# Lower parts of the weights and S5's two products move from GpSimd to VectorE in a one-core mixer kernel

## The chip, the core and the metric

The kernel runs on one core of a Trainium2 chip. The core has several engines, each with a queue of its own that it works off in order: TensorE multiplies matrices (PE in the profile's rows, PEld for its weight loads), VectorE (DVE) and ScalarE (ACT) do elementwise work, GpSimd (POOL) does elementwise work as well, and SyncE (SP) issues transfers. The metric is the device time of one execution in microseconds (us); lower is better. Times of one kernel are compared by the median of several runs.

## The reference

Two layers run one after the other on 512 tokens of width 1024. The first is a mixer of an S5 state-space branch and a gated convolution, followed by a squared-ReLU MLP. The second is a gated delta rule (forward and backward, with a context of 256 tokens) beside a Fourier mixer, followed by a mixture of 32 experts. What matters here is the first mixer and the dense products with its weights:

```python
proj = jnp.einsum('bsd,de->bse', xn, w_in) + b_in
u_ssm, c_bgate, c_cgate, c_val, g_ssm, g_conv = jnp.split(proj, SPLIT_POINTS, axis=-1)
y_ssm = s5_branch(u_ssm, ...)            # complex diagonal recurrence along the tokens
z = jax.nn.gelu(y_ssm)
y_a = (z @ w_glu_a) * jax.nn.sigmoid(z @ w_glu_b)
y_b = (c_bgate * causal_short_conv(c_cgate * c_val, conv_w, conv_b)) @ w_conv_out
merged = jax.nn.sigmoid(g_ssm) * y_a + jax.nn.sigmoid(g_conv) * y_b
return merged @ w_out
```

S5 has 32 groups of 64 complex states, 2048 states in all. The kernel does the complex recurrence as a rotation and two real scans: inputs are turned by cos and sin of the state's phase, scanned with a real decay, and turned back. The turning back takes four products per tile: sr = cos·zr − sin·zi and si = cos·zi + sin·zr.

## The kernel before, in words

Activations lie with features on the 128 partitions and the 512 tokens along the row. A dense product goes through its weights in blocks of 128 output columns (`dense`, with the weights from `weights`). Each fp32 weight block of 128x1024 is split in two: ScalarE casts it to a high part `wh` (L125), and `lsub` subtracts that from the block and so makes the low part `wl` (L126). TensorE then runs 24 matmuls per block: activations' high and low parts against `wh` (L130, L131) and the high part against `wl` (L138). `wh` and `wl` have two buffers each, and the loaded block `w`, which holds two blocks of 128 columns, has two as well. `lsub` is VectorE in most of the kernel. It is GpSimd in two stages: from the start of S5 until S5 is drained and its pools are closed, and from the start of `x_path` (the second layer's projections, its delta rule and its output projection) to the end.

S5 (`s5`) is a generator of 16 steps j, each for a tile of 128 states, with three pieces per step. `dense` calls for the next piece after its blocks (`fill`): two pieces after each block of the gate and value projections, one after a block of the bg projection and of the convolution's output projection, none in the gc blocks that come last. A piece's work goes to these lines: phase `fr` on VectorE (L442, L445, L446), its sin and cos on ScalarE (L448 to L450), two matmuls `bu` (L455), then VectorE's turning (L460 to L465) and scans (L468, L469), and the turning back (L473 to L478), of which L474 and L477 are on GpSimd. After each fourth step, 16 matmuls `y` (L486) read the four steps' sr and si. Beside it VectorE does the convolution of the gated branch (L547 to L557) and the low parts of its activations (L153).

In the second layer the lower parts are made beside the convolution taps of the projections (L1248) and a matrix inverse (L887 to L930), both on VectorE.

The order of the instructions on each engine is not written out by hand: a scheduler sets it when the program is built, and it moves instructions of independent pieces past one another.

Of the kernel before, what the change touches and what calls it, by code (L numbers as in the profile page):

```python
# [15 lines left out]
P = 128  # L16
# [13 lines left out]
def f(t):  # L30
    return t.bitcast(F32)
# [53 lines left out]
class Kern:  # L85
# [31 lines left out]
    def weights(self, w, r0, kt, c0, cols):  # L117
        nc = self.nc
        W = self.wp.tile([P, 8, 256], F32, tag="w", bufs=2, name=self.nm("w"))
        nc.sync.dma_start(  # L120
            W[:, :kt, :cols], w[r0:r0 + kt * P, c0:c0 + cols].rearrange("(k p) c -> p k c", p=P))
        for c in range(0, cols, P):
            H = self.wp.tile([P, 8, P], F32R, tag="wh", bufs=2, name=self.nm("wh"))
            L = self.wp.tile([P, 8, P], F32R, tag="wl", bufs=2, name=self.nm("wl"))
            nc.scalar.copy(H[:, :kt], W[:, :kt, c:c + P])  # L125
            self.lsub.tensor_sub(L[:, :kt], W[:, :kt, c:c + P], f(H[:, :kt]))  # L126
            yield H, L

    def accH(self, ps, H, aH, aL, k, sl=slice(None)):
# [85 lines left out]
    def setup(self):  # L215
        nc = self.nc
        ins = self.ins
        self.cp = self.pool("const")
        self.wes = ExitStack()
        self.es.enter_context(self.wes)  # L220
        self.wp = self.pool("wts", es=self.wes, side="right")
        self.pp = self.pool("ps", space=PSUM, es=self.ppes)
        self.lsub = nc.vector
        pk = self.cp.tile([P, ins["c_pack"].shape[1]], F32, name="pk")
        ni = COFF["ident"][1]
        assert COFF["ident"][0] == 0
        nc.gpsimd.dma_start(pk[:, :ni], ins["c_pack"][:, :ni])
        self.c = {k: pk[:, o:o + n] for k, (o, n) in COFF.items()}
        self.ident = self.c["ident"]
        self.ones = self.cp.tile([P, P], F32, name="ones")  # L230
        nc.vector.memset(self.ones, 1.0)
        self.pk = pk
# [195 lines left out]

    def s5(self, sp, u, zH, zL):
        nc = self.nc  # L430
        V, G = nc.vector, nc.gpsimd
        S = [P, T]

        def t(tag, bufs=1):
            return sp.tile(S, F32, tag=tag, bufs=bufs, name=self.nm(tag))

        st = {}
        for j in range(16):

            fr = t("fr")  # L440
            n = t("m1")
            V.tensor_tensor(fr.rearrange("p (a b) -> p a b", b=16),  # L442
                            self.fa[:, j, :32].unsqueeze(2).broadcast_to([P, 32, 16]),
                            self.fa[:, j, 32:].unsqueeze(1).broadcast_to([P, 32, 16]), op=ALU.add)
            V.tensor_scalar(n, fr, MAGIC, MAGIC, op0=ALU.add, op1=ALU.subtract)  # L445
            V.tensor_sub(fr, fr, n)  # L446
            sn, cs = t("sn", 2), t("cs", 2)
            nc.scalar.activation(sn, fr, AF.Sin, scale=2 * math.pi * (1 - 2e-7))  # L448
            nc.scalar.activation(fr, fr, AF.Abs)
            nc.scalar.activation(cs, fr, AF.Sin, scale=-2 * math.pi, bias=self.halfpi)  # L450
            jr = slice(32 * (j % 4), 32 * (j % 4) + 32)
            bu = []
            for i in range(2):
                b = self.pp.tile(S, F32, tag="q", bufs=4, name=self.nm("bu"))
                nc.tensor.matmul(b, self.bbT[jr, i, j // 4], u[jr, j // 4], start=True, stop=True,  # L455
                                 tile_position=(32 * (j % 4), 0))
                bu.append(b)
            yield
            m1, m2, m3, m4 = t("m1"), t("m2"), t("m3"), t("m4")
            V.tensor_mul(m1, cs, bu[0])  # L460
            V.tensor_mul(m4, sn, bu[0])
            V.tensor_mul(m2, sn, bu[1])
            V.tensor_mul(m3, cs, bu[1])
            V.tensor_add(m1, m1, m2)
            V.tensor_sub(m3, m3, m4)  # L465
            zr, zi = m2, m4
            mg = self.mag[:, j:j + 1].broadcast_to(S)
            V.tensor_tensor_scan(zr, mg, m1, 0.0, op0=ALU.mult, op1=ALU.add)  # L468
            V.tensor_tensor_scan(zi, mg, m3, 0.0, op0=ALU.mult, op1=ALU.add)  # L469
            yield  # L470
            sr, si = t("sr", 4), t("si", 4)
            n1, n2 = m1, m3
            V.tensor_mul(sr, cs, zr)  # L473
            G.tensor_mul(n1, sn, zi)  # L474
            V.tensor_sub(sr, sr, n1)
            V.tensor_mul(si, cs, zi)
            G.tensor_mul(n2, sn, zr)  # L477
            V.tensor_add(si, si, n2)  # L478
            st[j % 4] = (sr, si)
            if j % 4 == 3:  # L480
                i4 = j // 4
                y = self.pp.tile(S, F32, tag="q", bufs=4, name=self.nm("y"))
                for i in range(2):
                    for a in range(4):
                        ja = slice(32 * a, 32 * a + 32)
                        nc.tensor.matmul(y[ja, :], self.ccT[:, i, i4, ja], st[a][i], start=(i == 0), stop=(i == 1),  # L486
                                         tile_position=(0, 32 * a), skip_group_check=True)
                ys = t("m1")
                z = t("m2")
                V.scalar_tensor_tensor(ys, u[:, i4], self.v["ssm_d"][:, i4:i4 + 1], y, op0=ALU.mult, op1=ALU.add)  # L490
                nc.scalar.activation(z, ys, AF.Gelu_apprx_tanh)
                self.split(z, zH[:, i4], zL[:, i4])
            yield

    def block1(self):
        nc, ins = self.nc, self.ins
        V, A = nc.vector, nc.scalar
# [24 lines left out]
        sp = self.pool("s5", es=es)  # L522
        zz = a2.tile([P, 2, 4, T], F32R, tag="Z", name="zz")
        zH, zL = zz[:, 0], zz[:, 1]
        self.lsub = nc.gpsimd
        self.fillers.append(self.s5(sp, u, zH, zL))

        cH = ap_.tile(B, F32R, tag="D", name="cH")
# [45 lines left out]
        self.dense(w_in, xH, xL, take_gc, 4608, D)  # L574
        self.drain_fillers()
        es.close()
        self.lsub = nc.vector
        lp = tp = self.pool("late", es=aes)
        ya = lp.tile(B, F32, tag="G", name="ya")
        st = {}  # L580
# [53 lines left out]
        zr = tp.tile([P, D], F32, name="zr")  # L634
# [536 lines left out]
    def x_path(self):  # L1171

        nc, ins = self.nc, self.ins
        V, A, M, Q = nc.vector, nc.scalar, nc.tensor, nc.gpsimd
# [6 lines left out]
        w = ins["w_in_2"][0]  # L1181
        cw = self.v["conv_w_2"]
        x2d = self.dr.tile([P, KD, T], F32, name="x2d")
        self.lsub = Q

        def y_():
            return hp.tile([P, T], F32, tag="sq", bufs=3, name=self.nm("y"))
# [5 lines left out]
        G = self.cp.tile([P, 8], F32, name="gx")  # L1193
# [949 lines left out]
```

## Time and profile before

| what | value |
|---|---|
| median of 3 runs | 1989.0 us (1984.17 to 1991.39) |
| profiled execution, its own time | 1987.15 us |
| its span on the core | 1985.4 us |
| mean granted TensorE clock | 0.932 |
| TensorE busy | 1765.2 us, 89% of the span |
| VectorE busy | 1114.9 us, 56% |
| ScalarE busy | 585.3 us, 29% |
| GpSimd busy | 321.8 us, 16% |

All busy times are of the one profiled execution. They are means over stages that have different limits: the S5 stage lies at about 85 to 392 us of the span, the gc blocks after it end at about 430 us, the second layer's projections and delta rule lie at about 1030 to 1242 us, its output projection at about 1342 to 1400 us, and the experts after that.

### The profile page before, as it was taken

Reading aid. Unit: us, or ns where it says so; the run is one execution under the profiler, and the core shown is the slowest. Engines: PE = TensorE matmul, PEld = TensorE weight load, DVE = VectorE, ACT = ScalarE, POOL = GpSimd, SP = SyncE. Lnnn points to the kernel's source line nnn. Section 1 sums busy time; section 2 is a strip of 40 time slices with the busy share of each in tenths; the row PEclk is TensorE's granted clock in tenths of the full one; section 3 lists DMA queues with packets and bytes.
Section 4 is the critical chain, followed back from the end, with each engine's and each line's share of the span. In section 5 each row is a group of like instructions: output and inputs, shape, how many; then the busy total and the mean of one; then the engine's idle time right before and its main releaser. Section 6 shows DMA issues by size and latency. Waiting matters only on the chain. (4 is left out here: it accounts for less than half of the span.)

```text
span 1985.4 us, 24482 instructions
## 1 busy us (share of the span) xinstructions
PE 1765.2 (89%) x9169; PEld 1143.1 (58%) x9169; DVE 1114.9 (56%) x2231; ACT 585.3 (29%) x989; POOL 321.8 (16%) x210
## 2 busy tenths in 40 slices
PE   6778889699999999999998988999698898899985
PEld 4545556376676788777775665887333333333332
DVE  4889898833454665594466689573532323233225
ACT  3222324242343244332344633233411111111112
POOL 0434344420000000000012222003110111111000
PEclk9888889799999999999998889899799999999997
DMA  4111111138556333222231211006599999989993
GB/s 137 63 64 43 43 64 64 42 126 280 210 170 242 120 95 115 67 86 85 64 105 65 64 43 56 13 12 245 206 382 413 413 402 413 389 309 413 412 406 136
DMA packets 150266, 351.15 MB, mean 177 GB/s; under 512 B 20435, under 2 KB 107036, under 8 KB 130235
## 3 DMA queue, kind: packets, MB, share of 16 engines
q1 hardware_dynamic: 135533, 302.52, 41.2%
q0 software_dynamic: 9008, 33.58, 4.6%
q10 hardware_dynamic: 5534, 12.54, 1.7%
q8 instruction: 115, 1.88, 0.4%
q14 instruction: 76, 0.62, 0.1%
HBM read 339.63 MB, written 19.15 MB: 181 GB/s over the span
## 5 line engine op out<-in xcount | busy, mean ns | idle before, releaser
L125 ACT CAST wh<-w 128x1024 fp32r<-128x1024 f32 (+1 forms) x184 | 179.3, 975 | 407.7 <-PE acc L131 340.2
L126 POOL TENSOR_TENSOR wl<-w,wh 128x1024 fp32r<-128x1024 f32 (+1 forms) x76 | 184.7, 2434 | 621.0 <-PE acc L138 375.7
L1733 PE MATMUL gu<-ew,moe 128*64 128x512 f32 x1024 | 262.5, 639 | 14.2 <-DMA ew<-in_w_gate_dram 8.7
L126 DVE TENSOR_TENSOR wl<-w,wh 128x1024 fp32r<-128x1024 f32 (+1 forms) x108 | 123.2, 1141 | 118.7 <-PE acc L138 89.2
L1733 PEld LDWEIGHTS gu<-ew,moe 128*64 128x64 f32 x1024 | 73.9, 145 | 147.8 <-issue 120.4
L130 PE MATMUL acc<-xH,wh 128*128 128x512 f32 x352 | 151.3, 430 | 0.3 <-ACT wh L125 0.3
L131 PE MATMUL acc<-xL,wh 128*128 128x512 f32 x352 | 148.0, 420 | 0.0
L1742 DVE TENSOR_TENSOR moe<-gu,moe 64x512 f32<-64x512 f32 x32 | 21.8, 683 | 201.7 <-ACT moe L1741 136.2
L1758 PE MATMUL dn<-ew,hT 128*64 128x512 f32 x512 | 119.0, 608 | 0.5 <-ACT hT L1751 0.5
L130 PE MATMUL acc<-fH,wh 128*128 128x512 f32 x256 | 103.5, 405 | 0.4 <-ACT fH L152 0.4
L130 PE MATMUL acc<-gH,wh 128*128 128x512 f32 x256 | 103.2, 403 | 0.0
L1751 ACT COPY hT<-tr 128x128 f32<-128x128 f32 x64 | 13.9, 269 | 299.1 <-PE tr L1748 283.3
L131 PE MATMUL acc<-fL,wh 128*128 128x512 f32 x256 | 102.0, 398 | 0.0
L131 PE MATMUL acc<-gL,wh 128*128 128x512 f32 x256 | 102.0, 398 | 0.0
L138 PE MATMUL acc<-xH,wl 128*128 128x512 f32 x352 | 94.4, 412 | 6.5 <-DVE wl L126 3.7
L130 PEld LDWEIGHTS acc<-xH,wh 128*128 128x128 f32 x352 | 71.7, 204 | 42.3 <-issue 19.4
L1703 POOL DMA_INDIRECT yd<-moe,sx x31 | 32.0, 1033 | 339.2 <-DVE moe L1766 168.9
L131 PEld LDWEIGHTS acc<-xL,wh 128*128 128x128 f32 x352 | 71.5, 203 | 21.1 <-issue 5.5
L138 PEld LDWEIGHTS acc<-xH,wl 128*128 128x128 f32 x352 | 69.0, 197 | 24.0 <-DVE wl L126 4.2
L1758 PEld LDWEIGHTS dn<-ew,hT 128*64 128x64 f32 x512 | 36.4, 139 | 68.7 <-issue 63.8
L1766 DVE SCALAR_TENSOR_TENSOR moe<-dn,wv,moe 128x512 f32<-128x512 f32 x32 | 24.0, 751 | 89.5 <-PE dn L1758 64.6
L130 PE MATMUL acc<-hxH,wh 128*128 128x512 f32 x160 | 70.9, 447 | 2.1 <-DVE y L1248 2.1
(706 smaller groups left out, 3458.7 us busy)
## 6 DMA issues: line engine op xcount, KB each, us to landing
ew<-in_w_up_dram SPq DMA_DIRECT2D x64, 1024.0 KB
ew<-in_w_gate_dram SPq DMA_DIRECT2D x64, 1024.0 KB
ew<-in_w_down_dram SPq DMA_DIRECT2D x64, 1024.0 KB
w<-in_w_in_dram SPq DMA_DIRECT2D x36, 1024.0 KB
w<-in_w_ff_dram SPq DMA_DIRECT2D x32, 1024.0 KB
wm<-in_w_mod_dram POOLq DMA_DIRECT2D x24, 1024.0 KB, 6.5
xt<-in_x_dram SPq DMA_DIRECT2D x8, 512.0 KB
w<-in_w_conv_out_dram SPq DMA_DIRECT2D x4, 1024.0 KB
```

Of the source, the lines that this page charges most:

```text
L125: nc.scalar.copy(H[:, :kt], W[:, :kt, c:c + P])
L126: self.lsub.tensor_sub(L[:, :kt], W[:, :kt, c:c + P], f(H[:, :kt]))
L130: self.nc.tensor.matmul(ps, H[:, k], aH[:, k, sl], start=(k == 0), stop=False)
L131: self.nc.tensor.matmul(ps, H[:, k], aL[:, k, sl], start=False, stop=False)
L138: nc.tensor.matmul(ps, L[:, k], aH[:, k, sl], start=False, stop=(k == kt - 1))
L1703: nc.gpsimd.indirect_dma_start(out=self.yd.rearrange("r (m c) -> (r m) c", m=m), out_offset=bass.IndirectOffsetOnAxis(ap=sx, axis=0), in_= ...
L1733: mm = M.matmul(gu[64 * j:64 * j + 64], xs[:, k, s0:s0 + 64], ws[2 * (k // 4) + j][:, k % 4], start=(n == 0), stop=(n == 7), tile_position ...
L1742: V.tensor_mul(gh[:64], gu[:64], gh[64:])
L1751: put(hT[:, q:q + 2], pt[:, 64 * q:64 * q + 128].rearrange("p (k s) -> p k s", k=2))
L1758: M.matmul(dn[64 * j:64 * j + 64], hT[:, q], ws[4 + q // 2][:, q % 2, 512 * j:512 * j + 512], start=(q == 0), stop=(q == 3), tile_position ...
L1766: V.scalar_tensor_tensor(y, dn, wsl, m5, op0=ALU.mult, op1=ALU.mult)
```

## The change

All lower parts are made by VectorE: `lsub` is gone. In S5 the products L474 and L477 go to VectorE too. That moves 76 lower parts (60 of 128x1024 elements, 16 of 128x512) and 32 products of 128x512 from GpSimd to VectorE. Nothing is removed or added, and no buffer changes its size. In the changed kernel the line numbers are one lower in `s5`, two lower in the first layer after it, and three or four lower in the second.

```diff
             nc.scalar.copy(H[:, :kt], W[:, :kt, c:c + P])
-            self.lsub.tensor_sub(L[:, :kt], W[:, :kt, c:c + P], f(H[:, :kt]))
+            nc.vector.tensor_sub(L[:, :kt], W[:, :kt, c:c + P], f(H[:, :kt]))
             yield H, L
...
-        self.lsub = nc.vector
         pk = self.cp.tile([P, ins["c_pack"].shape[1]], F32, name="pk")
...
-        V, G = nc.vector, nc.gpsimd
+        V = nc.vector
...
             V.tensor_mul(sr, cs, zr)
-            G.tensor_mul(n1, sn, zi)
+            V.tensor_mul(n1, sn, zi)
             V.tensor_sub(sr, sr, n1)
             V.tensor_mul(si, cs, zi)
-            G.tensor_mul(n2, sn, zr)
+            V.tensor_mul(n2, sn, zr)
             V.tensor_add(si, si, n2)
...
-        self.lsub = nc.gpsimd
         self.fillers.append(self.s5(sp, u, zH, zL))
...
         es.close()
-        self.lsub = nc.vector
         lp = tp = self.pool("late", es=aes)
...
         x2d = self.dr.tile([P, KD, T], F32, name="x2d")
-        self.lsub = Q
```

The first place is VectorE's queue in the S5 stage, from a step's second scan to the next steps' first products. Names are tiles with the number of their use: `sr`, `si` are the step's results, `sn`, `cs` its sin and cos, `m_...` its scratch, `fr` the next step's phase, `magk` the decay, `wl`, `w` and `wh` low part, block and high part. A row ends with the engines that the instruction waits for. Before:

```order
L469 SCALAR_TENSOR_TENSOR m_214_1236<-magk,m_213_1235 128x512 [waits DVE_49]
L473 TENSOR_TENSOR sr_1278<-cs_1193,m_212_1234 128x512 [waits DVE_49]
L476 TENSOR_TENSOR si_1279<-cs_1193,m_214_1236 128x512 [waits DVE_49]
L475 TENSOR_TENSOR sr_1278<-sr_1278,m_211_1233 128x512 [waits DVE_49,Pool_49]
L478 TENSOR_TENSOR si_1279<-si_1279,m_213_1235 128x512 [waits DVE_49,Pool_49]
L442 TENSOR_TENSOR fr_1286<-fa 128x512
```

GpSimd's queue before, around the same step:

```order
L126 TENSOR_TENSOR wl_1429<-w_1366,wh_1428 128x1024 [waits PE_49,Activation_49]
L474 TENSOR_TENSOR m_211_1233<-sn_1192,m_214_1236 128x512 [waits DVE_49,Activation_49,Pool_49]
L477 TENSOR_TENSOR m_213_1235<-sn_1192,m_212_1234 128x512 [waits Pool_49]
L126 TENSOR_TENSOR wl_1487<-w_1484,wh_1486 128x1024 [waits DMAHW5_49,PE_49,Activation_49]
L126 TENSOR_TENSOR wl_1531<-w_1484,wh_1530 128x1024 [waits PE_49,Activation_49]
```

VectorE's queue in the changed kernel, at the same step:

```order
L468 SCALAR_TENSOR_TENSOR m_214_1236<-magk,m_213_1235 128x512 [waits DVE_49]
L472 TENSOR_TENSOR sr_1278<-cs_1193,m_212_1234 128x512 [waits DVE_49]
L473 TENSOR_TENSOR m_211_1233<-sn_1192,m_214_1236 128x512 [waits DVE_49]
L475 TENSOR_TENSOR si_1279<-cs_1193,m_214_1236 128x512
L474 TENSOR_TENSOR sr_1278<-sr_1278,m_211_1233 128x512 [waits DVE_49]
L476 TENSOR_TENSOR m_213_1235<-sn_1192,m_212_1234 128x512
L441 TENSOR_TENSOR fr_1286<-fa 128x512
L477 TENSOR_TENSOR si_1279<-si_1279,m_213_1235 128x512 [waits DVE_49]
L444 TENSOR_SCALAR m_223_1287<-fr_1286 128x512 [waits DVE_49]
L126 TENSOR_TENSOR wl_1369<-w_1366,wh_1368 128x1024 [waits DMAHW4_49,PE_49]
L445 TENSOR_TENSOR fr_1286<-fr_1286,m_223_1287 128x512 [waits DVE_49]
L126 TENSOR_TENSOR wl_1429<-w_1366,wh_1428 128x1024 [waits PE_49,Activation_49]
```

The two products now stand between the step's other products, the waits for GpSimd are gone, and two lower parts stand behind the step, ahead of the next step's turning. They wait for TensorE (the buffer of the low part) and for ScalarE (the high part).

The second place is VectorE's queue in the delta rule, where steps of the inverse (`inv`) alternate with convolution taps (`y`, from `pad` and the tap's weight in `vt`). Before:

```order
L916 TENSOR_TENSOR inv_7657<-inv_7657 128x252 [waits DVE_49]
L1248 SCALAR_TENSOR_TENSOR y_8280<-pad_7117,vt_538,y_8280 128x512 [waits DVE_49]
L918 TENSOR_TENSOR inv_7657<-inv_7657 128x18x14 [waits DVE_49]
L1248 SCALAR_TENSOR_TENSOR y_8280<-pad_7117,vt_538,y_8280 128x512 [waits DVE_49]
L916 TENSOR_TENSOR inv_7657<-inv_7657 128x255 [waits DVE_49]
```

In the changed kernel:

```order
L913 TENSOR_TENSOR inv_7657<-inv_7657 128x252 [waits DVE_49]
L1244 SCALAR_TENSOR_TENSOR y_8280<-pad_7117,vt_538,y_8280 128x512 [waits DVE_49]
L915 TENSOR_TENSOR inv_7657<-inv_7657 128x18x14 [waits DVE_49]
L1244 SCALAR_TENSOR_TENSOR y_8280<-pad_7117,vt_538,y_8280 128x512 [waits DVE_49]
L913 TENSOR_TENSOR inv_7657<-inv_7657 128x255 [waits DVE_49]
L126 TENSOR_TENSOR wl_8400<-w_8346,wh_8399 128x1024 [waits PE_49,Activation_49]
```

A lower part now stands in the inverse's chain and waits there for TensorE and ScalarE.

## Rows read from the trace of the kernel before

**Rows 1.** The page's 40 slices of the span, busy tenths of two engines.

```profile
DVE  4889898833454665594466689573532323233225
POOL 0434344420000000000012222003110111111000
```

**Rows 2.** Windows: stretch, its length, each engine's busy time with instructions, and more.

```profile
core 0: us, PE busy (x) PEld busy (x) DVE busy (x) ACT busy (x) POOL busy (x), PEclk, DMA share, GB/s
45.00:85.00 40.00, 29.28 (x112) 19.96 (x111) 30.16 (x113) 10.02 (x12) 11.36 (x4) 0.86 0.22 74
85.00:316.00 231.00, 187.34 (x639) 119.50 (x638) 212.43 (x230) 58.98 (x77) 97.66 (x46) 0.86 0.17 54
316.00:362.00 46.00, 44.22 (x175) 32.15 (x174) 39.31 (x35) 17.89 (x25) 22.35 (x10) 1.00 0.20 68
362.00:392.00 30.00, 14.47 (x45) 7.46 (x45) 27.59 (x26) 8.17 (x11) 14.22 (x7) 0.69 0.11 36
392.00:430.00 38.00, 37.18 (x151) 28.43 (x148) 15.14 (x12) 16.60 (x19) 14.55 (x9) 0.93 0.31 112
1030.00:1150.00 120.00, 104.29 (x436) 73.38 (x435) 80.50 (x184) 59.57 (x100) 30.67 (x12) 0.84 0.19 64
1150.00:1242.00 92.00, 76.82 (x420) 56.69 (x422) 87.02 (x142) 30.66 (x46) 26.33 (x11) 0.94 0.17 53
1342.00:1400.00 58.00, 55.90 (x260) 42.53 (x259) 21.23 (x32) 17.55 (x29) 21.64 (x18) 0.94 0.60 212
```

**Rows 3.** What TensorE waits for at 85 to 392: total us, times, longest.

```profile
PE y L486 <- DVE sr L475: 27.2, 7, 7.6
PE bu L455 <- DVE m L461: 13.3, 4, 6.4
```

**Rows 4.** Timeline of VectorE and GpSimd at 213 to 218: start, duration, instruction.

```profile
213.83 1.75 DVE L475 TENSOR_TENSOR sr<-sr,m 128x512 f32<-128x512 f32 x1
215.50 2.86 DVE L478 TENSOR_TENSOR si<-si,m 128x512 f32<-128x512 f32 x1
...
213.32 1.71 POOL L477 TENSOR_TENSOR m<-sn,m 128x512 f32<-128x512 f32 x1
214.99 2.82 POOL L126 TENSOR_TENSOR wl<-w,wh 128x1024 fp32r<-128x1024 f32 x1
```

**Rows 5.** VectorE's groups at 85 to 392: busy us, mean ns | idle before.

```profile
L478 DVE TENSOR_TENSOR si<-si,m 128x512 f32<-128x512 f32 x16 | 39.1, 2442 | 0.0
L475 DVE TENSOR_TENSOR sr<-sr,m 128x512 f32<-128x512 f32 x16 | 28.2, 1760 | 1.2 <-POOL m L474 1.2
L476 DVE TENSOR_TENSOR si<-cs,m 128x512 f32<-128x512 f32 x16 | 27.2, 1701 | 0.0
...
L469 DVE TENSOR_TENSOR_SCAN m<-magk,m 128x512 f32<-128x512 f32 x16 | 19.1, 1195 | 0.0
...
L461 DVE TENSOR_TENSOR m<-sn,bu 128x512 f32<-128x512 f32 x16 | 10.9, 679 | 0.0
```

**Rows 6.** GpSimd's groups at 85 to 392.

```profile
L126 POOL TENSOR_TENSOR wl<-w,wh 128x1024 fp32r<-128x1024 f32 x31 | 82.8, 2676 | 72.1 <-PE acc L138 42.7 <-ACT wh L125 21.5 <-ACT m L491 6.9
L477 POOL TENSOR_TENSOR m<-sn,m 128x512 f32<-128x512 f32 x16 | 27.1, 1695 | 0.0
```

**Rows 7.** VectorE's lower parts at 430 to 1000, where `lsub` is VectorE.

```profile
L126 DVE TENSOR_TENSOR wl<-w,wh 128x1024 fp32r<-128x1024 f32 x83 | 101.3, 1220 | 92.2 <-PE acc L138 68.8 <-ACT wh L125 21.3 <-PE acc L287 2.1
```

**Rows 8.** VectorE's groups in the delta rule at 1150 to 1242.

```profile
L1248 DVE SCALAR_TENSOR_TENSOR y<-pad,vt,y 128x512 f32<-128x512 f32 x39 | 35.2, 902 | 0.0
...
L887 DVE TENSOR_TENSOR m<-m,beta 128x1024 f32<-128x1024 f32 x2 | 4.5, 2309 | 0.0
L1248 DVE SCALAR_TENSOR_TENSOR y<-pad,vt,acc 128x512 f32<-128x512 f32 x6 | 4.4, 738 | 2.2 <-PE acc L1246 2.2
L904 DVE SCALAR_TENSOR_TENSOR inv<-m,pk,inv 128x512 f32<-128x512 f32 x2 | 3.5, 1786 | 0.0
...
L888 DVE TENSOR_TENSOR m<-m,pk 128x1024 f32<-128x1024 f32 x2 | 2.3, 1212 | 0.0
```

## The prediction

> **What bounds the kernel now.** I read the 40 slices first, to see where the two engines of the change are busy together. GpSimd works in slices 2 to 9, where VectorE stands at 8 or 9 tenths, in slices 21 to 25, and lightly after that [rows 1]. So the change touches three stretches, and the mean VectorE share of the table (56%) says nothing about them. The windows give each stretch its limit [rows 2]. At 85 to 316 us, the S5 loop, VectorE is busy 212.4 of 231 us and TensorE 187.3. At 316 to 362 TensorE has 44.2 of 46: it sets the pace there. At 362 to 392, when the projections have run ahead and only S5 is left, VectorE has 27.6 of 30 and TensorE 14.5. At 392 to 430 TensorE has 37.2 of 38. In the delta rule, at 1150 to 1242, VectorE has 87.0 of 92 and TensorE 76.8; at 1030 to 1150 neither is full (80.5 and 104.3 of 120); at 1342 to 1400 TensorE has 55.9 of 58. TensorE's waits in the S5 stage say the same: 27.2 us of them end with VectorE's `sr` and 13.3 us with VectorE's turning, which frees the buffer that the next `bu` is written to [rows 3].
>
> So VectorE binds in two of the S5 stretches and in the delta rule, and the change gives it more to do there. What decides is how much of its busy time is work. The groups answer that [rows 5]. L461, a product of 128x512 with one input in PSUM, takes 679 ns. L476, L475 and L478 are also one product, one difference and one sum of 128x512, and take 1701, 1760 and 2442 ns, without idle time ahead of them. In the timeline L475 ends at 215.58 and GpSimd's L477 at 215.03; L478 ends at 218.36 and GpSimd's lower part at 217.81 [rows 4]. Both times VectorE's instruction ends 0.55 us after GpSimd's, as if it could begin only when GpSimd had finished. I read this as VectorE being held while GpSimd reads the memory that both use, if VectorE's own instruction takes two operands from there; L461, with an operand in PSUM, is not held.
>
> [...]
>
> **The change part by part.** Prices first. A lower part on VectorE takes 1.220 us [rows 7], against 2.676 on GpSimd [rows 6]. A product takes 0.68 us (L461), against 1.695. An instruction starts about 0.08 us before the one ahead ends (L475 starts at 213.83, lasts 1.75, and L478 starts at 215.50), so what one adds to VectorE's queue is 1.14 and 0.60 us.
>
> Added in the S5 stage: 31 lower parts and 32 products (two in each of 16 steps; 63 GpSimd instructions in the three windows together). That is 31 x 1.14 + 32 x 0.60 = 35.3 + 19.2 = 54.5 us.
>
> Removed there: the held time. The three slow groups alone have 39.1 + 28.2 + 27.2 - 3 x 10.9 = 61.8 us of it. For all groups I take VectorE's busy time less what its instructions would take unheld: 0.60 us each, and 0.52 more for each of the 32 scans (1.195 against 0.68). This is an estimate, since a few instructions are shorter or longer. At 85 to 316: 212.4 - 230 x 0.60 - 24 x 0.52 = 62. At 316 to 362: 39.3 - 35 x 0.60 - 4 x 0.52 = 16. At 362 to 392: 27.6 - 26 x 0.60 - 4 x 0.52 = 10. Together 88 us.
>
> The net by stretch, GpSimd's instructions being 22 lower parts and 24 products in the first, 6 and 4 in the second, 3 and 4 in the third:
> At 85 to 316: 25.1 + 14.4 = 39.5 added, 62 removed, net -22.5. TensorE has 43.7 idle us there to let the loop shorten.
> At 316 to 362: 9.2 added, 16 removed; net -7 for VectorE, but TensorE is the limit. I take 0.
> At 362 to 392: 5.8 added, 10 removed, net -4. TensorE only waits there.
> At 392 to 430: five lower parts, 5.7 us, into 22.9 us that VectorE is idle. 0; with no cover +6.
> At 45 to 85, the preparation of S5: four lower parts, 4.6 us, into 9.8 idle us of VectorE. 0, bounds -4 (some instructions held there too) and +5.
>
> The delta rule. At 1150 to 1242 there are nine lower parts, 10.3 us. Held: taps L1248 take 902 ns against 738 for those with an operand in PSUM, 39 x 0.164 = 6.4; L887 2 x (2.309 - 1.212, by L888 of the same size) = 2.2; L904 2 x (1.786 - 0.738) = 2.1; 10.7 in all [rows 8]. The inverse has other instructions that look drawn out, which I don't count. I take -2, with bounds of -8 and +10 (all nine on the path, nothing given back). At 1030 to 1150 there are eight, 9.1 us, beside 39.5 idle us of VectorE: 0, and +9 without that cover. The output projection at 1342 to 1400 has the 16 half-sized ones and one whole, below 17 x 1.14 = 19.4 us, beside 36.8 idle us: 0.
>
> What else moves. No transfer is added and no queue of transfers is passed. But a lower part now stands in VectorE's queue with S5's instructions behind it, and waits there for ScalarE's cast and for TensorE to free the buffer; before, GpSimd waited alone. In the new order they stand mostly between a step's phase and its turning, where VectorE waited for sin and cos anyway. How long they will wait the trace of before cannot show. It is bounded by 0 and by 1.11 us each, the idle time ahead of a lower part where VectorE makes them now (92.2 / 83) [rows 7]. I take a value near 0, because in that stretch VectorE has nothing else to do and so idles without cost, while in S5 it is the late one and finds its buffers free.
>
> The sum: -22.5 - 4 - 2 = -28.5 us on the profiled execution's 1987.15, which makes 1958.7. That execution lies 1.85 us under the median of 1989.0, so the same against the median is 1960.5; I say 1959. The experts behind it are limited by transfers that start with the output projection (transfers' share 0.60 there), and I take it that they move ahead as a whole.
>
> **The rivals.**
> (1) The loop gains, but half of it is lost again. TensorE's matmuls against the low part now depend on the engine that is late, where GpSimd made them early; a wait of TensorE for `wl` takes the place of that for `sr`. GpSimd's only 2.676 us speak for it, since `wl` was rarely late before. 0.5 us for each of 22 lower parts is 11 us: -28.5 + 11 = -17.5, and with the delta rule at +5 instead of -2, -10: about 1978.
> (2) Slower: VectorE blocks. If each lower part of S5 and the projections (31 + 17) waits 1.11 us at the head of the queue with the recurrence behind it, that is 53 us, and the result +25: about 2013. The point from which it decides is 28.5 / 48 = 0.6 us each. For it: 42.7 us of GpSimd's idle time ahead of its lower parts end with TensorE's matmuls and 21.5 with ScalarE's cast [rows 6], so they do arrive just behind these. Against it: GpSimd took each as soon as it could, VectorE comes to them later.
> (3) GpSimd takes real load off a full engine, and the slow VectorE instructions are slow for another reason. Then 31 x 1.22 + 32 x 0.68 = 59.6 us come on top in S5: about 2045. Against it are the two ends 0.55 us apart and L461. [...]
> (4) More gain. The lower parts fill the gaps in which VectorE waits for sin and cos, so that its 18.6 idle us at 85 to 316 shrink too, say by 13, and the second stretch and the delta rule give their full -7 and -8: -22.5 - 13 - 7 - 4 - 8 = -54.5, about 1934.
>
> **How the numbers follow.** My forecast (a gain of 18 to 45 us): 0.57. Rival 1: 0.19, half of it faster by over 0.5% (10 us, about what a measurement of this kernel can tell from no change) and half within. Rival 2: 0.14, of which 0.11 by more than 10 us. Rival 3: 0.03. Rival 4: 0.07. Faster: 0.57 + 0.09 + 0.07 = 0.73; within: 0.10 + 0.03 = 0.13; slower: 0.14. The range leaves out most of rivals 3 and 4 and the upper end of rival 2: 1937 to 1990. My forecast's own is 1944 to 1971.
>
> **What would show it right or wrong.** Right: L475, L476 and L478 (one line lower then) at about 680 ns each; lower parts in S5 at about 1.2 us on VectorE; its busy time in the loop some 20 us less; TensorE's waits for `sr` and for the turning smaller by as much; the gc blocks reached some 26 us earlier. Rival 1 would show as TensorE waiting for `wl` from VectorE, rival 2 as VectorE idle ahead of L126 inside the loop, by TensorE or ScalarE. The forecast fails if the three groups stay at 1.7 us or more, if the loop stays as long with a shorter busy VectorE, or if the delta rule grows by as much as S5 gives.

## The result and the profile after

The changed kernel took 1919.8 us (median of 4 runs, 1917.9 to 1925.5) against 1990.2 for the kernel before on the same occasions. The ratio is 0.9651, with a 95% interval of 0.9616 to 0.9687: 70 us faster. The forecast was 1959 with a range of 1937 to 1990, so the time lies 17 us below the range. The direction was right, the size less than half of what came.

The changed kernel's slices, the same rows as [rows 1]:

```profile
DVE  4899999334545654864558797565432232232315
POOL 0000000000000000000000000000001011011100
```

The slices show GpSimd out of the S5 loop and of the delta rule, and the stretch in which VectorE is full has become shorter (six slices at 8 or 9 tenths, where there were seven).

To compare stage by stage I cut both traces at the same work: S5 from its first phase to its last `si`, and from there to the first product that reads S5's result. First the kernel before, then the changed one, in the windows view (columns as in [rows 2]):

```profile
79.10:393.00 313.90, 252.17 (x878) 162.73 (x877) 283.45 (x296) 89.33 (x118) 137.49 (x64) 0.87 0.17 54
393.00:433.90 40.90, 40.84 (x164) 31.54 (x165) 14.14 (x12) 17.22 (x20) 14.10 (x8) 0.95 0.29 104
```

```profile
74.60:332.40 257.80, 230.48 (x860) 152.89 (x858) 245.31 (x357) 87.29 (x114) 0.00 (x0) 0.94 0.19 62
332.40:374.10 41.70, 41.70 (x177) 32.65 (x176) 14.06 (x18) 18.45 (x22) 2.00 (x3) 1.00 0.37 128
```

VectorE runs 61 instructions more in the S5 loop and is busy 38 us less. It is idle 12.5 us there, where it was idle 30.4. The loop is 56 us shorter. Where the profiled executions' 61.7 us of difference in span come from, by the same cuts: 4.5 us ahead of S5's first phase, 56.1 in the loop, -0.8 in the gc blocks behind it, 0.5 up to the second layer's first product, 10.3 from there to the output projection, and -8.9 (given back) in the output projection and the experts. That last stretch lasts 644 to 654 us from one profile to another in the runs below, with the changed kernel and with kernels that change nothing in it, so I don't count its difference as an effect; the medians, 70 us apart, are nearer to the 70.6 gained up to there.

The groups that answer to [rows 5], one line lower now, and the lower parts beside them:

```profile
L126 DVE TENSOR_TENSOR wl<-w,wh 128x1024 fp32r<-128x1024 f32 x30 | 36.4, 1216 | 1.3 <-PE acc L138 1.3
...
L468 DVE TENSOR_TENSOR_SCAN m<-magk,m 128x512 f32<-128x512 f32 x16 | 19.1, 1196 | 0.0
...
L475 DVE TENSOR_TENSOR si<-cs,m 128x512 f32<-128x512 f32 x16 | 10.9, 681 | 0.0
L474 DVE TENSOR_TENSOR sr<-sr,m 128x512 f32<-128x512 f32 x16 | 10.9, 681 | 0.0
L477 DVE TENSOR_TENSOR si<-si,m 128x512 f32<-128x512 f32 x16 | 10.9, 681 | 0.0
```

The product, the difference and the sum take 681 ns each, where they took 1701, 1760 and 2442. The lower parts took the price forecast. What TensorE waits for in the loop, as in [rows 3]:

```profile
PE acc L138 <- DVE wl L126: 20.4, 7, 8.8
PE y L485 <- DVE sr L474: 5.3, 3, 4.7
PE bu L454 <- DVE m L489: 0.8, 1, 0.8
```

The waits for `sr` and the turning are nearly gone. In part a wait for the lower part has taken their place, as rival 1 said, but it does not set the pace: VectorE does, with 245 of 258 us.

In the second layer, the groups that answer to [rows 8]; this view reaches from the first projection to the end of the delta rule, so it has 76 taps in place of 39:

```profile
L1244 DVE SCALAR_TENSOR_TENSOR y<-pad,vt,y 128x512 f32<-128x512 f32 x76 | 55.6, 744 | 0.4
L126 DVE TENSOR_TENSOR wl<-w,wh 128x1024 fp32r<-128x1024 f32 x18 | 21.8, 1218 | 10.5 <-ACT beta L778 7.9 <-PE acc L138 2.6
...
L884 DVE TENSOR_TENSOR m<-m,beta 128x1024 f32<-128x1024 f32 x2 | 2.4, 1218 | 0.0
L901 DVE SCALAR_TENSOR_TENSOR inv<-m,pk,inv 128x512 f32<-128x512 f32 x2 | 1.4, 744 | 0.0
```

Taps 744 ns (854 over the same stretch before, 902 in the delta rule), L884 (L887 before) 1218 (2309), L901 (L904 before) 744 (1786).

### The profile page after: what moved, and what is told of

Same layout as the page of the kernel before. It is cut to its first block, busy times and chain, and to the rows that moved or that the text cites. A ratio compares the mean times of both kernels' runs of the same rounds, so it can differ in the third digit from the quotient of the medians.

```text
span 1923.7 us, 24386 instructions
## 1 busy us (share of the span) xinstructions
PE 1743.1 (91%) x9169; PEld 1133.1 (59%) x9169; DVE 1072.9 (56%) x2339; ACT 584.8 (30%) x988; POOL 84.0 (4%) x102
## 5 line engine op out<-in xcount | busy, mean ns | idle before, releaser
L126 DVE TENSOR_TENSOR wl<-w,wh 128x1024 fp32r<-128x1024 f32 (+1 forms) x184 | 207.1, 1126 | 151.2 <-PE acc L138 103.9
L130 PE MATMUL acc<-xH,wh 128*128 128x512 f32 x352 | 144.4, 410 | 0.0
L131 PE MATMUL acc<-xL,wh 128*128 128x512 f32 x352 | 141.4, 402 | 0.0
L130 PEld LDWEIGHTS acc<-xH,wh 128*128 128x128 f32 x352 | 67.4, 191 | 35.2 <-issue 12.6
L131 PEld LDWEIGHTS acc<-xL,wh 128*128 128x128 f32 x352 | 67.3, 191 | 17.8 <-issue 3.2
L131 PE MATMUL acc<-hxL,wh 128*128 128x512 f32 x160 | 66.3, 419 | 0.0
L138 PE MATMUL acc<-gH,wl 128*128 128x512 f32 x256 | 65.6, 398 | 0.0
```

Of the source, the lines that this page charges most:

```text
L126: nc.vector.tensor_sub(L[:, :kt], W[:, :kt, c:c + P], f(H[:, :kt]))
L130: self.nc.tensor.matmul(ps, H[:, k], aH[:, k, sl], start=(k == 0), stop=False)
L131: self.nc.tensor.matmul(ps, H[:, k], aL[:, k, sl], start=False, stop=False)
L138: nc.tensor.matmul(ps, L[:, k], aH[:, k, sl], start=False, stop=(k == kt - 1))
```

## The experiments

Two theories stood against each other. The first: VectorE is held while GpSimd reads the memory that both use, whoever needs GpSimd's result, and the time held is more than the work that GpSimd took over. The second: S5 waited for GpSimd's slow results, or it is the order of the instructions that counts, and holding plays no part. The first four runs split the change into its parts.

**Only the products on VectorE.**

```diff
-            G.tensor_mul(n1, sn, zi)
+            V.tensor_mul(n1, sn, zi)
...
-            G.tensor_mul(n2, sn, zr)
+            V.tensor_mul(n2, sn, zr)
```

> S5's two products on VectorE, all lower parts as before on GpSimd. Theory (VectorE is held while GpSimd reads the same memory): L475 and L476 fall from 1.70 and 1.76 us to about 0.68 unless a lower part of GpSimd falls beside them, L478 stays drawn out, since a lower part of 2.7 us comes just then; some 34 us of held time go and 19 us of work come: 10 to 20 us less than before. Rival (the lower parts on VectorE fill gaps in which it waited, and the products matter little): within 5 us of before.

Measured: 1948.9 us, ratio to before 0.9796 (0.9747 to 0.9844), 41 us less (31 to 50 by the interval). L476 and L475 fall to 815 and 679 ns, but L478 to 680 as well, where it was expected to stay drawn out.

**Only the S5 stage's lower parts on VectorE.**

```diff
-        self.lsub = nc.gpsimd
         self.fillers.append(self.s5(sp, u, zH, zL))
```

> The lower parts of the S5 stage on VectorE, products and the second layer's lower parts as before on GpSimd. Theory: L478 falls to about 0.7 us, L475 and L476 stay at 1.7; some 58 us of held time go and 35 us of work come, 20 to 30 us less than before, with about 10 more if VectorE's waits for ScalarE's sin and cos shrink because lower parts stand in them. Rival (lower parts at the head of VectorE's queue block it, the gain came from the products): no gain.

Measured: 1957.1 us, ratio 0.9834 (0.9803 to 0.9865), 33 us less. As expected, L478 falls, to 679 ns, and L475 and L476 stay drawn out (1687 and 1433).

**Both, the second layer as before** (the two edits above together).

> Products and lower parts of the S5 stage on VectorE, the second layer's lower parts as before on GpSimd. Theory: the S5 stage as in the changed kernel (gc blocks reached some 59 us earlier than before), the delta rule as before: about 7 us more than the changed kernel, 1925 to 1932. If the two parts are independent, the gain is that of e1 plus that of e2; if GpSimd's products and lower parts hold VectorE in turn, it is more.

Measured: 1927.9 us, ratio 0.9685 (0.9653 to 0.9716), 63 us less.

**Only the second layer's lower parts on VectorE.**

```diff
         x2d = self.dr.tile([P, KD, T], F32, name="x2d")
-        self.lsub = Q
```

> Only the second layer's lower parts on VectorE, S5 as before. Theory: taps, L887 and L904 of the delta rule at their unheld times, and 5 to 9 us less than before. Rival (lower parts in the inverse's chain wait for TensorE and ScalarE): no gain, or up to 10 us more.

Measured: 1982.0 us, ratio 0.9967 (0.9943 to 0.9991), 7 us less. In its trace the taps are at 746 ns and L887 at 1211.

What follows. Each part alone is a gain, the products more than I expected; the other three came within or near what was expected. 63 and 7 make up the whole 70. The products' and the lower parts' gains add up to 41 + 33 = 74 against 63, but the intervals are as wide as that difference, so whether they are additive is open. The S5 stage by the same cuts (us; the column on the right is when S5's result is first read):

| kernel | S5 loop | VectorE busy | idle | result first read at |
|---|---|---|---|---|
| before | 313.9 | 283.5 | 30.4 | 433.9 |
| only products | 298.4 | 259.6 | 38.8 | 401.8 |
| only lower parts | 276.2 | 254.6 | 21.6 | 398.2 |
| both | 257.7 | 245.3 | 12.4 | 375.4 |
| changed kernel | 257.8 | 245.3 | 12.5 | 374.1 |

(With only the products moved, half of the gc blocks run inside the loop, so there the right column is the one to compare.) Busy time falls with either part, but idle time falls only where the lower parts are on VectorE. The waits of VectorE show which idle time that is. Before:

```profile
DVE m L460 <- ACT cs L450: 9.3, 7, 3.0
DVE m L462 <- ACT sn L448: 5.9, 7, 2.0
```

Only products:

```profile
DVE m L460 <- ACT cs L450: 17.5, 9, 3.7
DVE m L462 <- ACT sn L448: 11.5, 9, 3.6
```

Changed kernel:

```profile
DVE m L459 <- ACT cs L449: 3.1, 4, 1.5
...
DVE m L461 <- ACT sn L447: 2.1, 1, 2.1
```

It is mostly the wait for sin and cos: 15.2 us before, 29.0 with only the products moved, 5.2 in the changed kernel. One of its places in the changed kernel, VectorE's and ScalarE's timelines:

```profile
187.84 0.68 DVE L445 TENSOR_TENSOR fr<-fr,m 128x512 f32<-128x512 f32 x1
188.44 1.22 DVE L126 TENSOR_TENSOR wl<-w,wh 128x1024 fp32r<-128x1024 f32 x1
189.61 0.69 DVE L461 TENSOR_TENSOR m<-sn,bu 128x512 f32<-128x512 f32 x1
...
188.95 0.63 ACT L447 ACTIVATE sn<-fr 128x512 f32<-128x512 f32 x1
```

The phase is ready at 188.52 and its sine at 189.58. The first product with it starts at 189.61, and the lower part fills the time between. I summed all 16 such intervals of each trace, from the end of the phase's last subtraction to the first product with sin or cos. Before, they are 27.6 us, 12.7 of them idle. In the changed kernel they are 28.8 us, of which 15.8 are lower parts (13 of 1.22 us) and 3.7 idle. With only the products moved 12.9 are idle, with only the lower parts moved 6.8. So 13 of the 30 lower parts in the loop stand in these intervals, and some 9 of their 15.8 us take the place of idle time. Counted to the last of the four products with sin or cos, it is 17 lower parts, and 22.7 us of idle time before against 9.2.

**Reading GpSimd work that nobody needs.** In the changed kernel, each step's `sr` and `si` start a product on GpSimd that reads a constant and whose result is read by nobody.

```diff
+        k = self.c["iota"]
+        def beside(s):
+            d = t("dd", 2)
+            V.tensor_copy(d[:, :1], s[:, :1])
+            nc.gpsimd.tensor_mul(d, k, k)
...
             V.tensor_sub(sr, sr, n1)
+            beside(sr)
...
             V.tensor_add(si, si, n2)
+            beside(si)
```

> The changed kernel with 32 products of 128x512 added on GpSimd, two in each S5 step: both operands are a constant in the memory that both engines use, the result is read by nobody. A VectorE copy of one column starts each. Theory (VectorE is held while GpSimd reads there, whoever needs the result): VectorE's two-operand instructions beside them rise to 1.5 to 2.4 us again, about 20 to 50 us of held time, the S5 loop 15 to 50 us longer than the changed kernel's 258. Rival (S5 was slow since it waited for GpSimd's products and lower parts, not since it was held): the loop within 8 us of 258, VectorE's durations as in the changed kernel.

**Writing GpSimd work that nobody needs.**

```diff
-            nc.gpsimd.tensor_mul(d, k, k)
+            for _ in range(3):
+                nc.gpsimd.memset(d, 0.0)
```

> The same with each product replaced by three fills of 128x512 with zeros on GpSimd, which write to that memory and read nothing, for about the same time. Theory: no instruction of VectorE that reads is drawn out, and the S5 loop is at 258 plus 3 to 8 us for the 32 small copies. If GpSimd's writes hold VectorE as well, it is as long as with the products.

Measured, one execution each: 1936.5 us with reads (S5 loop 273.8 us, VectorE busy 265.0 in it), 1928.4 with writes (259.8, 247.9), beside 257.8 and 245.3 without either. The changed kernel itself took 1913 to 1928 us in its executions, so the loop and not the whole time is to be compared. With reads, groups of VectorE and GpSimd in the loop:

```profile
L126 DVE TENSOR_TENSOR wl<-w,wh 128x1024 fp32r<-128x1024 f32 x31 | 43.2, 1396 | 1.4 <-PE acc L138 0.9 <-PE tp L272 0.5
...
L451 DVE TENSOR_TENSOR fr<-fr,m 128x512 f32<-128x512 f32 x16 | 17.1, 1068 | 0.1
...
L437 POOL TENSOR_TENSOR dd<-pk 128x512 f32<-128x512 f32 x31 | 57.8, 1879 | 290.6 <-DVE dd L436 202.7 <-PE bu L460 87.9
```

With writes:

```profile
L126 DVE TENSOR_TENSOR wl<-w,wh 128x1024 fp32r<-128x1024 f32 x33 | 40.3, 1223 | 5.6 <-PE acc L138 5.1 <-PE tp L272 0.5
...
L452 DVE TENSOR_TENSOR fr<-fr,m 128x512 f32<-128x512 f32 x16 | 11.0, 688 | 0.1
...
L438 POOL MEMSET dd<- 128x512 f32 x96 | 54.3, 573 | 281.5 <-DVE dd L436 189.8 <-PE bu L461 88.0
```

GpSimd is busy for much the same time, 57.8 and 54.3 us. Where it reads, VectorE's lower part rises to 1396 ns and the phase's subtraction to 1068, and VectorE is busy 17 us more. Where it only writes, both stay at their own 1223 and 688. Nobody waits for these results and the rest is the same, so it is the holding and not a wait for GpSimd. The loop is 16 us longer than the changed kernel's, at the lower edge of the 15 to 50 expected, and what is held, 17 us, is below the 20 to 50: most of VectorE's groups in the loop keep their time, those that fall beside the added products do not. It holds both ways: in the run with reads, around 211 to 214 us,

```profile
211.57 0.68 DVE L484 TENSOR_TENSOR si<-si,m 128x512 f32<-128x512 f32 x1
212.17 1.53 DVE L556 SCALAR_TENSOR_TENSOR cc<-vp,vt,cc 128x512 f32<-128x512 f32 x1
...
211.28 1.88 POOL L437 TENSOR_TENSOR dd<-pk 128x512 f32<-128x512 f32 x1 [11.32 <-DVE dd L436]
213.84 1.04 POOL L437 TENSOR_TENSOR dd<-pk 128x512 f32<-128x512 f32 x1 [0.69 <-DVE dd L436]
```

GpSimd's product takes 1.88 us beside VectorE's sum, which keeps its 0.68, and 1.04 us beside an instruction (L497) with an operand in PSUM, where this kernel keeps its matmuls' results (`y` here). VectorE's tap behind it is held until 213.70, 0.54 us after GpSimd's end, the distance that [rows 4] showed. So the reading of [rows 4] holds with a GpSimd instruction that has nothing to do with S5.

**Each lower part of the S5 stage made twice.**

```diff
-            nc.vector.tensor_sub(L[:, :kt], W[:, :kt, c:c + P], f(H[:, :kt]))
+            for _ in range(self.lows):
+                nc.vector.tensor_sub(L[:, :kt], W[:, :kt, c:c + P], f(H[:, :kt]))
...
+        self.lows = 2
         self.fillers.append(self.s5(sp, u, zH, zL))
...
         es.close()
+        self.lows = 1
```

> The changed kernel with each lower part made twice in a row in the S5 stage, the second writing the same again: 40 more instructions of 1.14 us on VectorE, some 30 of them in the S5 loop. If the lower parts' price on VectorE is 1.14 us each with VectorE the bound, the loop grows by 30 to 40 us. If they stand in gaps in which VectorE waits for ScalarE (rival 4 of the prediction), a part of the second ones fits there too and the loop grows by 15 to 25 us.

Measured, one execution: 1952.6 us, and the loop (windows view)

```profile
79.00:366.70 287.70, 241.63 (x853) 158.66 (x853) 275.63 (x385) 87.19 (x113) 0.00 (x0) 0.88 0.17 55
```

is 29.9 us longer with VectorE busy 30.3 us more. The loop holds 57 lower parts in place of 30, so 27 more cost 1.1 us each: the full price, and far from the price that gaps would give. VectorE's wait for sin and cos is 5.6 us, as it was (5.2). So VectorE bounds the changed loop, and the gaps were used up by the first ones.

**S5's pieces spread over the gc blocks.** The first attempt at a faster kernel: VectorE is nearly full in the loop and TensorE in the gc blocks behind it.

```diff
-            self.dense(w_in, xH, xL, take_cg, 1536 + i * P, 256, fill=2)
+            self.dense(w_in, xH, xL, take_cg, 1536 + i * P, 256, fill=1)
...
-        self.dense(w_in, xH, xL, take_gc, 4608, D)
+        self.dense(w_in, xH, xL, take_gc, 4608, D, fill=1)
```

> The changed kernel with S5's pieces spread over the gc blocks as well: one piece instead of two after each block of the gate projection, one instead of none after each gc block. The work is the same. In the changed kernel VectorE bounds the S5 loop (busy 245 of 258 us) and TensorE the gc blocks (40 of 40, VectorE 14.5). With both spread evenly the two stretches together, 300 us, come near 275: 15 to 25 us less than the changed kernel, 1895 to 1905. If it is ScalarE's sin and cos or the order that bounds the loop and not VectorE's work, the time stays within 5 us.

Measured: 1922.0 us, ratio to before 0.9673 (0.9639 to 0.9707), not to be told from the changed kernel; the 15 to 25 us expected did not come. The product that first reads S5's result begins at 356.3 us in place of 374.1, as expected; the second layer begins at 991.4 in place of 991.7. Some 17 of these 18 us are lost in between. TensorE's timeline there:

```profile
359.80 0.62 PE L485 MATMUL y<-sr,ccT 128*32 128x512 f32 x1 [0.43 <-DVE sr L474]
...
361.60 1.05 PE L485 MATMUL y<-si,ccT 128*32 128x512 f32 x2 [0.74 <-DVE si L477]
364.80 0.49 PE L130 MATMUL acc<-zz,wh 128*128 128x512 f32 x1 [2.15 <-ACT zz L152]
```

S5's last step now stands bare in front of the products that need all of it, and then matmuls wait for a transfer (6.3 us in all, for `wm`). At 365 to 381 us, after and between these waits, the mean granted clock is 0.63; over 356 to 426 us it is 0.90, against 1.00 over the 70 us from 374 in the changed kernel. A matmul that is issued every 0.23 us at 374 in the changed kernel comes every 0.43 us at 368 here. These are the three places I found; how much each has of the 17 us was not measured.

**Half of that spread.** S5 ends four gc blocks earlier than in the run above.

```diff
-            self.dense(w_in, xH, xL, take_cg, 1536 + i * P, 256, fill=2)
+            self.dense(w_in, xH, xL, take_cg, 1536 + i * P, 256, fill=2 - i // 2 % 2)
...
-        self.dense(w_in, xH, xL, take_gc, 4608, D)
+        self.dense(w_in, xH, xL, take_gc, 4608, 512, fill=1)
+        self.dense(w_in, xH, xL, lambda m, ps: take_gc(m + 4, ps), 5120, 512)
```

> As e8, but S5's last piece comes with the fourth gc block instead of the eighth: the gate projection asks for one piece instead of two after every other pair of blocks, and the first four gc blocks ask for one each. Theory (in e8 the S5 loop and the gc blocks together got 18 us shorter, and lost it again where S5's last step stood bare ahead of the next products): half of the 18 us are kept and nothing is lost behind it, 6 to 12 us less than the changed kernel. If something else takes the gain back (the transfers that the next stage waits for come at their own time), it is within 4 us of the changed kernel.

**The same with the first convolution tap on ScalarE.**

```diff
-                V.tensor_scalar(c, vp[:, 2:], cw[:, 16 + ch:17 + ch], cb[:, ch:ch + 1], op0=ALU.mult, op1=ALU.add)
+                A.activation(c, vp[:, 2:], AF.Identity, scale=cw[:, 16 + ch:17 + ch], bias=cb[:, ch:ch + 1])
```

> As e9, and the first tap of the gated branch's convolution on ScalarE (8 instructions of 0.54 us less for VectorE, 35% busy ScalarE takes them). If VectorE's work still bounds the loop, 3 to 4 us less than e9. If TensorE does by then, the same as e9.

**The changed kernel again, beside these two.**

> The changed kernel unaltered, beside e9 and e10 on the same chip: 1917 to 1923.

Measured: 1915.1 us (ratio to before 0.9615, 0.9589 to 0.9641), 1917.7 (0.9631, 0.9601 to 0.9660), and 1919.5 for the changed kernel (0.9638, 0.9607 to 0.9669). The half spread may be 4 us faster, short of the 6 to 12 expected; the intervals overlap, so that is open. The tap on ScalarE brings the first read of S5's result 3 us forward (367.9 against 371.0), as expected, and nothing that the times can tell.

## Why the prediction was right or wrong

**That VectorE is held** was right, and both sides of it were well sized. The forecast had 88 us held in the S5 stage and 54.5 us added. VectorE's busy time fell from 283.5 to 245.3; with 30 x 1.14 + 32 x 0.60 = 53.4 us of added work, what was held comes to 91.6. That all the time read as held would go was assumed in the forecast, and no row of before could show it; the three groups at 681 ns bear it out. The reading was too narrow in one point, which the 88 us, counted over all groups, did not depend on: instructions with a single tensor were held too (the first tap took 923 ns before and 540 after, last section).

**The step that failed is the way from VectorE's busy time to the length of the loop.** The forecast took 26.5 us from a net of 33.5, and the loop gave 56.1. The 29.6 us between are 17.9 us of idle time, the 7 us of the stretch that was set to 0, and 4.7 us by which the net was larger. Two places of the prediction:

- It took the loop's gain from busy time alone, so VectorE's idle time was to stay. It went from 30.4 to 12.5 us. 13.5 of these 17.9 us went between the phase and the last product with sin or cos, where 17 lower parts now stand; the rest went from several smaller waits. The order shown ahead of the prediction had it, and the text said so in the paragraph on what else moves, but used it only as a reason to take their waits near 0, not as a gain. Rival 4 had this step right and priced it at 13 us, with the two stretches at their full value, and got a chance of 0.07. Its 1934 was the nearest of the cases.
- "At 316 to 362: 9.2 added, 16 removed; net -7 for VectorE, but TensorE is the limit. I take 0." But at 362 to 392 only S5 was left, as the prediction says itself, so what VectorE saves earlier leaves less of S5 for that end. The runs bear this out: in the last 31 us of the loop TensorE is busy 14.7 us before and 30.4 in the changed kernel, and all of the 38 us of busy time came off the loop. In the changed kernel TensorE is as full at 280 to 332 us (51.8 of 52.4) while VectorE has 50.5, and the run with each lower part made twice says that VectorE sets the pace.

**The second layer** was mis-sized: -2 forecast, 10.3 measured in the profile, 7 in the times of the run with that part alone. The 0 for the stretch at 1030 to 1150 was right: counted from the second layer's first product, the inverse's first step (L887, L884) begins after 104.0 us before and 105.7 in the changed kernel, with nine lower parts and seven taps more on VectorE ahead of it, so the idle time there was cover. From that step to TensorE's first product with the finished inverse it is 84.4 us before and 74.4 after, VectorE busy 81.9 and 68.6. The forecast's -2 set nine lower parts there against three groups of 10.7 us. It lacked the inverse's own steps (66 instructions `inv` from `inv`, 32.8 us before and 27.6 after), which it named and did not count, and the seven taps that now stand ahead; and of the lower parts seven stand in that stretch, not nine.

**The preparation of S5**, taken as 0 with a bound of -4: the first phase came 4.5 us earlier in the changed kernel's profile and 3.1 in that of the two runs with all of S5's part or its lower parts; 1.3 of the 4.5 is there at the first matmul already, where both kernels are the same. At the bound, and small.

**Rival 1** (TensorE waits for the lower part): the wait exists, 20.4 us, but the pace of the loop is VectorE's, which is busy 245 of 258 us. **Rival 2** (VectorE blocks): VectorE waited 1.3 us in all ahead of L126 in the loop, against the 34 us that it would have taken. **Rival 3** is excluded by the run with reads against the one with writes (its sum makes 2047 to 2049, not 2045).

Not settled is why the products alone gave 41 us where the held time of their two groups, less their own work, had let me expect 10 to 20. In its profile S5's result is read 32 us earlier, so a part of the 41 may be spread of the times. In that run the sum after them is at 680 ns as well, though the lower parts are still on GpSimd, and the hold by these has moved to other instructions (the second scan L469 from 1195 to 1596 ns, a tap L551 from 745 to 1487) and become less in all. Without the products ahead of it GpSimd no longer works without a break beside VectorE's turning back, which would explain it; I did not test that alone.

## What to carry to other kernels

Elementwise work on GpSimd beside a full VectorE cost VectorE more here than it took off it (busy 283.5 us in the S5 loop with that work on GpSimd, 245.3 with it on VectorE itself): compare a VectorE instruction of the same shape in a stretch without GpSimd before believing a busy share. A full VectorE in a trace is a reason to ask how much of the time is held (some 92 of 283.5 us here), and what is given back should be counted with the waits that the moved instructions can stand in. A stretch in which TensorE is full (44.2 of 46 us here) inside a stage that ends with another engine's work need not be a limit: add up the bounding engine's queue over the whole stage.

## What the runs showed that I had not expected

GpSimd that only writes (96 fills, 54.3 us) left VectorE's mean durations nearly as they were, with one exception below; GpSimd that reads (31 products, 57.8 us) cost VectorE 17 us. GpSimd was held in turn: the same product took 1.04 us beside an instruction with an operand in PSUM and 1.88 beside VectorE's two-operand sum, so its durations in that stage are not its own. VectorE instructions that take a single tensor were held too: the first tap of the gated branch, `cc` from `vp`, took 923 ns in the mean before and 540 after. So were small ones: L196 of the second layer, with 128x32 elements, took 2.27 us before and 0.16 after, and L784, of the same size, 1.05 and 0.18 (L781 there). The first tap is also the exception: beside the fills it took 774 and 773 ns in two of its eight cases and 537 to 591 in the others.
